# Hybrid decoder layer, recurrent branch: keys of head h+2 made beside the scan of head h, a longer planned inverse, three weight pairs, and the combination held back

## The chip, the cores and the metric

One NeuronCore of one Trainium2 chip runs one program: a whole decoder layer for 1024 tokens of width 1024, in float32. The metric is device time in microseconds (us), from the start of the execution to its end. The kernel before takes 2791.61 us, the median of three runs (2788.59 to 2793.04).

Five engines are spoken of. TensorE (PE) multiplies matrices, and loads its weights in a row of its own (PEld). VectorE (DVE) and ScalarE (ACT) work elementwise and read what TensorE leaves in PSUM. GpSimd (POOL) does little here. SyncE (SP) issues the DMAs. Each engine works through its instructions in the order of its own queue.

## The reference

```python
x = x + 0.5 * swiglu(rmsnorm(x, ffn1_norm), ...)
h = rmsnorm(x, mix_norm)
# h @ w_in gives, side by side:
#   q, k, v of branch A: attention in 3 groups of 4 heads of 64, dilations 1, 4, 16
#   q, k, v of branch B: gated delta rule, 8 heads of 128, after a causal convolution of 4 taps and silu
#   beta and decay of each head of B, the output gate of B, two merge gates
merged = sigmoid(gate_a) * (ya @ w_branch_a) + sigmoid(gate_b) * (yb @ w_branch_b)
x = x + merged @ w_out
x = x + 0.5 * swiglu(rmsnorm(x, ffn2_norm), ...)
out = rmsnorm(x, final_norm)
```

In branch A the three groups' outputs are joined by a softmax over their log-denominators. In branch B, for each head and each chunk of tokens,

```python
M = where(tri_strict, (k * beta) @ k.T * decay, 0)
u, w = solve(I + M, [v * beta, k * beta * exp(gcum)])      # unit lower triangular
# then over the chunks in turn
v_new = u - w @ state
o     = q_dec @ state + (q @ k.T * decay) @ v_new
state = state * state_dec + k_dec.T @ v_new
```

and `o` is normalised and gated. Every float32 product with a weight matrix is computed as three products of rounded parts (xH*wH + xL*wH + xH*wL).

## The kernel before, in words

**Stages.** `ffn1`, then `mixer` (attention first, then the eight recurrent heads), then `merge_out` (branch products, gates, w_out), then the second SwiGLU. `layer` runs them in order and opens the memory pools that lie between them.

**Projections.** `proj` (L206) multiplies one tile of 128 columns of `w_in` with half of the tokens: 24 matmuls of 128x512, so 48 for a tile. `load_w` (L182 to L184) brings a weight tile: a DMA into `wraw`, a ScalarE cast into `wH`, a VectorE subtraction into `wL`. Two `wraw` and four pairs of `wH` and `wL` are held.

**The planner.** In the mixer the order of TensorE's instructions is written out at build time and kept. `Weave` holds a clock in planned us: each TensorE instruction adds its planned cost (0.23 for a 128x512 matmul, 0.22 for a 128x128 one, 0.11 for a transpose). Tasks are Python generators: where one yields a number, it is due again that many planned us later. Projections are the filler: after every 2.07 planned us of them (`STRETCH`) the tasks that are due put their instructions into TensorE's stream. If an operand isn't there yet on the chip, TensorE waits; it can't take another instruction first. For the other engines a scheduler sets the order at build time by rank: attention and the combination first ("att"), then the heads in their order, then the projections ("bulk").

**A head** X of branch B goes through these tasks:

- `gdn_keys`: projection, then `gdn_conv` (ScalarE L910, L917, L920, VectorE L919), 8 planned us after each half `by_token` (transposes at L926, sum of squares L936 and L937). It starts `gdn_decay`, too.
- `gdn_decay`: the decay tile D (matmuls L993, Exp L995), of which there is one buffer. It waits until the head before has both halves of its values and its product A, and while a step of the combination is open.
- `gdn_solve`: scales D, 6 planned us later makes the products N (L1009, put out by VectorE at L1011), then `gdn_inverse_blocks`. That inverts 32x32 blocks on VectorE: N goes to DRAM and comes back into `Tm` (L1068), 60 small dependent steps (L1077, L1078, with L1090 and L1091 between), DRAM and back into `U` (L1099, L1104), a transpose into `Tm` (L1106). `Tm` has one buffer. `yield INVERSE - 5.0` and a further `yield 5.0` are the planned time of all this; INVERSE is 48.
- `gdn_merge` joins the blocks with small matmuls (L1126, L1133, L1143, L1151), a STRETCH between them; then w (L1051), then the scan.
- `gdn_queries`, `gdn_values`, `gdn_gate`: a projection each. The values' transposes wait until the head before has put out its output (`final`); once `U` is there the values are multiplied by it (L1179), which sets `solved`.
- `gdn_scan`: eight chunks in turn (L1218, L1222, L1228, L1235), a STRETCH between steps; after chunks 4 and 8 `gdn_output` is started, which 10 planned us later transposes and stores half an output.

A tile `ka` holds 128x1024; keys, scaled keys, queries, N, A, decayed keys and w of a head each take one, of nine in all.

**The combination** (`combine`) joins the attention groups in eight steps, one per 128 tokens: a dozen VectorE instructions, two transposes 12 planned us later (L866), a copy (L869). It begins 8 planned us after attention has ended, and each step waits while segments of a decay tile are open or while more than one started head lacks its values.

**The work list** in `mixer`: keys, queries, values of head 0; then for each h keys and queries of h+1, the gate of h, values of h+1, one merge gate tile. The first entry is taken once `free` says so: keys of h when head h-2 is `scanned`, the gate of h when h-1 is final, values of h when h-1 has its values. Until then one of the 16 merge gate tiles is taken as filler; when there are none, `idle` moves the clock on.

Of the kernel before, what the change touches and what calls it, by code (L numbers as in the profile page):

```python
# [9 lines left out]
F32 = mybir.dt.float32  # L10
# [6 lines left out]
P = 128  # L17
# [4 lines left out]
NT = T // P  # L22
# [46 lines left out]
def psum(C, tag):  # L69
    return C.pp.tile([P, 512], F32, name=tag, tag=tag, bufs=BANKS[tag])  # L70


@contextmanager
def band(C, name):

    saved = C.tc.cur_priority
    C.tc.cur_priority = C.bands[name]
    yield
    C.bands[name] = C.tc.cur_priority
    C.tc.cur_priority = saved  # L80
# [54 lines left out]

TILES = {"ka": 9, "xp": 2, "U": 2, "Tm": 1, "g": 1}


def t4(C, tag, dt=F32):
    return C.mx.tile([P, T + {"Tm": 32, "xp": 16}.get(tag, 0)], dt, name=tag, tag=tag, bufs=TILES[tag])

# [686 lines left out]
def combine(C):  # L830

    nc = C.nc
    while not C.attended:
        yield 1.0
    yield 8.0
    for t in range(NT):

        while C.segs or sum(not X.vals[1] for X in C.heads) > 1:
            yield 1.0
        C.combining = True  # L840
        oc = C.tp.tile([P, 792], F32, name="oc", tag="xs", bufs=2).rearrange("p (g q f) -> p g q f", g=3, q=2)
        for g in range(3):
            nc.sync.dma_start(oc[:, g], C.od[g][t * P:t * P + P])
        m, l = oc[:, :, :, 128:130], oc[:, :, :, 130:132]
        M = C.mx.tile([P, 1, 2, 2], F32, name="cM", tag="cM", bufs=2)
        e = C.mx.tile([P, 3, 2, 2], F32, name="ce", tag="ce", bufs=2)
        z = C.mx.tile([P, 3, 2, 2], F32, name="cz", tag="cz", bufs=2)
        nc.vector.tensor_tensor(out=M, in0=m[:, 0:1], in1=m[:, 1:2], op=ALU.max)
        nc.vector.tensor_tensor(out=M, in0=M, in1=m[:, 2:3], op=ALU.max)
        nc.vector.tensor_tensor(out=e, in0=m, in1=M.to_broadcast([P, 3, 2, 2]), op=ALU.subtract)  # L850
        nc.scalar.activation(e, e, AF.Exp, scale=0.125)
        nc.vector.tensor_tensor(out=z, in0=e, in1=l, op=ALU.mult)
        nc.vector.tensor_tensor(out=M, in0=z[:, 0:1], in1=z[:, 1:2], op=ALU.add)
        nc.vector.tensor_tensor(out=M, in0=M, in1=z[:, 2:3], op=ALU.add)
        nc.vector.reciprocal(M, M)
        nc.vector.tensor_tensor(out=e, in0=e, in1=M.to_broadcast([P, 3, 2, 2]), op=ALU.mult)
        for q in range(2):
            ov = oc[:, :, q, 0:128].rearrange("p g (h d) -> p g h d", d=64)
            nc.vector.tensor_tensor(out=ov, in0=ov, in1=e[:, :, q, :].unsqueeze(3).to_broadcast([P, 3, 2, 64]), op=ALU.mult)
        y = oc[:, 0, :, 0:128]  # L860
        for g in (1, 2):
            nc.vector.tensor_tensor(out=y, in0=y, in1=oc[:, g, :, 0:128], op=ALU.add)
        yield 12.0
        ps = psum(C, "tA")
        for f in range(2):
            C.weave.pe(nc.tensor.transpose(ps[:, f * P:f * P + P], y[:, f, :], C.ident), 0.11)  # L866
        C.combining = False
        yT = C.mx.tile([P, 2, P], F32, name="yT", tag="sc", bufs=6)
        nc.scalar.copy(yT, ps[:, :256].rearrange("p (f t) -> p f t", t=P))  # L869
        nc.sync.dma_start(C.yad[:, :, t * P:t * P + P], yT)  # L870
# [14 lines left out]
class Head:  # L885
# [7 lines left out]
        self.solved, self.scanned = [False] * 2, False  # L893

    @property
    def band(self):
        return f"h{self.h}"

# [41 lines left out]


def gdn_keys(C, w_in, X):
    X.ssq = C.mx.tile([P, 16], F32, name="gssq", tag="gssq", bufs=2)
    X.cl = C.mx.tile([P, 5, NT], F32, name="cl", tag="cl", bufs=2)
    X.k, X.kd = t4c(C, "ka"), t4c(C, "ka")

    def then(q):
        by_token(C, X, X.k, q, 0, X.kd)
        if q:
            yield from gdn_solve(C, X)  # L950

    C.weave.add(in_band(C, X.band, gdn_decay(C, X)), 0.0)
    gdn_conv(C, w_in, C_KB + X.h * P, 8 + X.h, X, X.k, then)
# [19 lines left out]
def gdn_decay(C, X):  # L973


    nc = C.nc
    h = X.h
    while C.combining or X.prev and not (X.prev.vals[1] and X.prev.A):
        yield 0.6
    C.segs = True  # L980
    segs = []
    for q in range(2):
        sg = C.tp.tile([P, 2, 4, P], F32R, name="seg", tag="xs", bufs=2)
        for i, gx in enumerate((C.gH, C.gL)):
            for c in range(4):
                nc.scalar.activation(sg[:, i, c, :], C.incl, AF.Copy, scale=gx[:, q * 4 + c, h:h + 1].bitcast(F32))
        segs.append(sg)
    yield 8.0
    D = C.tp.tile([P, NT, P], F32, name="Dm", tag="gB", bufs=1)
    for q, sg in enumerate(segs):  # L990
        ps = psum(C, "tA")
        for i in range(2):
            C.weave.pe(nc.tensor.matmul(ps, C.strictR, sg[:, i].rearrange("p c t -> p (c t)"), start=i == 0, stop=i == 1), 0.23)  # L993
        d = D[:, q * 4:q * 4 + 4, :]
        nc.scalar.activation(d, ps.rearrange("p (c t) -> p c t", t=P), AF.Exp)  # L995
        nc.gpsimd.affine_select(out=d, in_=d, pattern=[[0, 4], [1, P]], compare_op=ALU.is_ge, fill=0.0,
                                base=0, channel_multiplier=-1)
    X.D, C.segs = D, False


def products(C, X, src, sign):

    nc = C.nc
    dst = t4c(C, "ka")
    for q in range(2):
        ps = psum(C, "tA")
        for i in range(4):
            c = q * 4 + i
            C.weave.pe(nc.tensor.matmul(ps[:, i * P:i * P + P], X.k[:, c, :], src[:, c, :], start=True, stop=True), 0.22)  # L1009
        cs = slice(q * 4, q * 4 + 4)  # L1010
        nc.vector.scalar_tensor_tensor(dst[:, cs, :], ps.rearrange("p (c t) -> p c t", t=P), sign, X.D[:, cs, :],  # L1011
                                       op0=ALU.mult, op1=ALU.mult)
    return dst


def gdn_solve(C, X):

    nc = C.nc
    h = X.h
    while X.D is None:  # L1020
        yield 0.6
    rs, sv = rsqrt_cols(C, X.ssq[:, 0:8], 1.0, EPS, 8, "rg", w=24)
    s, nk, ks = [X.cl[:, i] for i in range(3)]
    nc.vector.tensor_tensor(out=s, in0=rs, in1=rs, op=ALU.mult)
    nc.vector.tensor_tensor(out=s, in0=s, in1=C.beta[:, :, h], op=ALU.mult)
    for q in range(2):
        d = X.D[:, q * 4:q * 4 + 4, :]
        nc.vector.tensor_tensor(out=d, in0=d, in1=s[:, q * 4:q * 4 + 4].unsqueeze(2).to_broadcast([P, 4, P]), op=ALU.mult)
    nc.vector.tensor_tensor(out=nk, in0=rs, in1=sv, op=ALU.mult)
    nc.vector.tensor_tensor(out=ks, in0=s, in1=C.eS[:, :, h], op=ALU.mult)  # L1030
    X.nk = nk
    yield 6.0
    X.N = products(C, X, X.k, -1.0)
    Tm, Um = gdn_inverse_blocks(C, X)
    yield INVERSE - 5.0
    while X.A is None:
        yield 0.6

    kg = t4c(C, "ka")
    for dst, sc in ((kg, C.eG[:, :, h]), (X.kd, ks)):  # L1040
        for q in range(2):
            cs = slice(q * 4, q * 4 + 4)
            nc.vector.tensor_tensor(out=dst[:, cs], in0=X.kd[:, cs], in1=sc[:, cs].unsqueeze(2).to_broadcast([P, 4, P]), op=ALU.mult)
    yield 5.0
    yield from gdn_merge(C, X, Tm, Um)

    X.w = t4c(C, "ka")
    for q in range(2):
        ps = psum(C, "tA")
        for i in range(4):  # L1050
            C.weave.pe(nc.tensor.matmul(ps[:, i * P:i * P + P], kg[:, q * 4 + i, :], X.U[:, q * 4 + i, :], start=True, stop=True), 0.22)  # L1051
        nc.scalar.copy(X.w[:, q * 4:q * 4 + 4, :], ps.rearrange("p (c t) -> p c t", t=P))
    yield STRETCH
    yield from gdn_scan(C, X)
# [99 lines left out]
    yield STRETCH  # L1154


INVERSE = 48.0


def gdn_values(C, w_in, X):  # L1160
# [133 lines left out]
def mixer(C, tc, I):  # L1294
# [9 lines left out]
    with tc.tile_pool(name="mx", bufs=1) as C.mx:  # L1304
# [39 lines left out]

        def free(what, h):
            if what is keys:
                return h < 2 or heads[h - 2].scanned
            if what is gdn_gate:
                return h < 1 or heads[h - 1].final[1]
            return what in (gdn_queries, gate_tile) or h < 1 or heads[h - 1].vals[1]  # L1350

        while work or gates:
            if work and free(*work[0]):
                what, h = work.pop(0)
# [78 lines left out]
            turn()  # L1433


def open_pools(C, tc, st):
    C.wbufs = (2, 4)
    C.wp = st.enter_context(tc.tile_pool(name="wp", bufs=1, reuse_waits="tile"))
    C.tp = st.enter_context(tc.tile_pool(name="tp", bufs=2, reuse_waits="tile"))


def layer(tc, I, out):
    C = Kern()
# [3 lines left out]
    with ExitStack() as st:  # L1447
# [19 lines left out]
            C.hL[a] = hp.tile([P, KT, 512], F32R, name=f"hL{a}")  # L1467

        ffn1(C, tc, I, open_h)
        open_pools(C, tc, st)  # L1470
        mixer(C, tc, I)
        C.pool_split = False
        with tc.tile_pool(name="x2", bufs=1) as xp2:
            x2 = xp2.tile([P, NT, D], F32, name="x2")
# [79 lines left out]
```

## Time and profile before

| | |
|---|---|
| three runs, us | 2788.59, 2791.61, 2793.04 |
| profiled execution, own time, us | 2792.52 |
| its span, first to last instruction, us | 2790.6 |
| mean granted TensorE clock | 0.976 |
| first SwiGLU, us of the span | 0 to 735 |
| attention | 735 to 1010 |
| recurrent heads (the last attention blocks run into it) | 1010 to 1850 |
| merge_out | 1850 to 2060 |
| second SwiGLU | 2060 to 2790 |

How to read the views that follow. The page's first part gives busy time, share of the span and count of instructions for each engine. The view by stretches gives one row per stretch of the span, in us from its start: its length, then for PE, PEld, DVE, ACT and POOL the busy time with the count in brackets, then the TensorE clock granted (1.00 is full speed), the busy share of the DMA engines, and GB/s. In the list of waits a row says which instruction of an engine waited for which other instruction: total us, times, longest. In the timeline a row is a run of like instructions: start, length, engine, line, operation, tiles written and read, shapes, count, and in square brackets the idle time before and what ended it. In a list of groups the figures behind the count are busy us, mean ns of one, and idle us before.

### The profile page before, as it was taken

The numbers are of one execution on the slowest core, as the hardware profiler recorded it, in microseconds if no ns is written. First come the engines' busy times: TensorE is split into PE (matmuls) and PEld (weight loads), VectorE is DVE, ScalarE is ACT, GpSimd is POOL, SyncE is SP. The second block draws the span as 40 slices with busy tenths as digits, with TensorE's granted clock in tenths as the row PEclk, the third lists the DMA queues.
The fourth block names the chain that finished last, engine by engine and source line by source line (L and its number), as shares of the span: only waits on it lengthen the run. The fifth ranks groups of instructions, "written<-read, shape, count | busy, mean of one in ns | idle before, by whom it ended". The sixth has DMA issues, their size and how long they took to land. (4 is left out here: it accounts for less than half of the span.)

```text
span 2790.6 us, 34448 instructions
## 1 busy us (share of the span) xinstructions
PE 2652.4 (95%) x13223; PEld 2199.6 (79%) x13223; DVE 1371.2 (49%) x3238; ACT 920.3 (33%) x1574; POOL 300.1 (11%) x256
## 2 busy tenths in 40 slices
PE   6999999999799998799899899999999999999998
PEld 5888887887688787687788777888778888888886
DVE  6443434434453458667667587345553232232325
ACT  5333332212343456344244443253441111111112
POOL 5544442001100000000000000000010000000002
PEclk9999999999899999899999999999999999999999
DMA  4322324421332222222212122255421111111111
GB/s 145 105 69 87 91 80 149 145 91 61 99 89 60 60 76 63 69 71 66 56 41 55 50 67 77 66 173 166 159 83 46 46 53 53 46 46 50 46 55 61
DMA packets 276997, 221.20 MB, mean 79 GB/s; under 512 B 38144, under 2 KB 226784, under 8 KB 276832
## 3 DMA queue, kind: packets, MB, share of 16 engines
q1 hardware_dynamic: 276832, 219.00, 26.1%
q8 instruction: 104, 1.70, 0.3%
q14 instruction: 61, 0.50, 0.1%
HBM read 173.76 MB, written 38.90 MB: 76 GB/s over the span
## 5 line engine op out<-in xcount | busy, mean ns | idle before, releaser
L206 PE MATMUL mm<-hH,wL 128*128 128x512 f32 x1440 | 589.9, 410 | 0.0
L206 PE MATMUL mm<-hL,wH 128*128 128x512 f32 x1440 | 567.5, 394 | 0.0
L206 PE MATMUL mm<-hH,wH 128*128 128x512 f32 x1440 | 567.4, 394 | 0.0
L183 ACT CAST wH<-wraw 128x1024 fp32r<-128x1024 f32 (+1 forms) x189 | 197.3, 1047 | 747.7 <-PE mm L206 328.4
L184 DVE TENSOR_TENSOR wL<-wraw,wH 128x1024 fp32r<-128x1024 f32 (+1 forms) x189 | 230.5, 1222 | 213.9 <-ACT wH L183 204.8
L206 PEld LDWEIGHTS mm<-hL,wH 128*128 128x128 f32 x1440 | 273.9, 190 | 60.7
L206 PEld LDWEIGHTS mm<-hH,wL 128*128 128x128 f32 x1440 | 274.1, 190 | 59.7 <-issue 6.0
L206 PEld LDWEIGHTS mm<-hH,wH 128*128 128x128 f32 x1440 | 274.8, 191 | 50.4
L206 PE MATMUL tC<-hH,wL 128*128 128x512 f32 x416 | 161.8, 389 | 0.0
L206 PE MATMUL tC<-hL,wH 128*128 128x512 f32 x416 | 161.8, 389 | 0.0
L206 PE MATMUL tC<-hH,wH 128*128 128x512 f32 x416 | 161.8, 389 | 0.0
L263 DVE TENSOR_TENSOR sg<-sg,tC 128x512 f32<-128x512 f32 x44 | 30.3, 688 | 247.9 <-PE tC L206 247.9
L239 POOL TENSOR_TENSOR xg<-x,gB 128x1024 f32<-128x1024 f32 x16 | 38.3, 2395 | 602.3 <-DVE x L1427 357.0
L387 DVE TENSOR_TENSOR wL<-wS,wH 128x1024 fp32r<-128x1024 f32 x44 | 63.3, 1438 | 79.2 <-ACT wH L386 77.9
L1482 POOL TENSOR_TENSOR y<-x,gB 128x1024 f32<-128x1024 f32 x8 | 19.1, 2388 | 706.3 <-DVE x L294 706.3
L206 PEld LDWEIGHTS tC<-hL,wH 128*128 128x128 f32 x416 | 78.1, 188 | 16.3
L206 PEld LDWEIGHTS tC<-hH,wL 128*128 128x128 f32 x416 | 78.2, 188 | 16.2
L206 PEld LDWEIGHTS tC<-hH,wH 128*128 128x128 f32 x416 | 78.0, 187 | 16.1
L919 DVE SCALAR_TENSOR_TENSOR ka<-xp,cw,ka 128x512 f32<-128x512 f32 x96 | 72.5, 755 | 13.1 <-ACT ka L917 11.9
L455 POOL TENSOR_TENSOR su<-su,sg 128x512 f32<-128x512 f32 x42 | 64.3, 1551 | 86.5 <-DVE su L429 76.7
L386 ACT CAST wH<-wS 128x1024 fp32r<-128x1024 f32 x44 | 46.3, 1052 | 78.1 <-PE tC L397 37.5
L568 PE MATMUL mm<-wH,hidH 128*128 128x512 f32 x176 | 69.3, 394 | 2.6 <-DVE x L570 1.8
(405 smaller groups left out, 5347.6 us busy)
## 6 DMA issues: line engine op xcount, KB each, us to landing
wraw<-in_w_in_dram SPq DMA_DIRECT2D x64, 512.0 KB, 4.0
wraw<-in_ffn_w_gate_dram SPq DMA_DIRECT2D x46, 512.0 KB, 3.9
wraw<-in_ffn_w_up_dram SPq DMA_DIRECT2D x46, 512.0 KB, 4.0
wraw<-in_ffn_w_down_dram SPq DMA_DIRECT2D x44, 512.0 KB, 3.6
wraw<-hd SPq DMA_DIRECT2D x22, 512.0 KB, 4.9
hd<-su SPq DMA_DIRECT2D x42, 256.0 KB, 3.2
wraw<-in_w_branch_b_dram SPq DMA_DIRECT2D x16, 512.0 KB, 4.3
wraw<-in_w_out_dram SPq DMA_DIRECT2D x16, 512.0 KB, 3.7
```

Of the source, the lines that this page charges most:

```text
L183: nc.scalar.copy(H[:, :width], raw[:, :width])
L184: (nc.gpsimd if C.pool_split else nc.vector).tensor_tensor(out=L[:, :width], in0=raw[:, :width], in1=H[:, :width].bitcast(F32), op=ALU.sub ...
L206: ins = nc.tensor.matmul(ps, w[:, k, :], x[:, k, :], start=k == 0 and i == 0, stop=k == kt - 1 and i == 2)
L239: nc.gpsimd.tensor_tensor(out=xs, in0=x_t, in1=gB, op=ALU.mult)
L263: nc.vector.tensor_tensor(out=sg, in0=sg, in1=pu, op=ALU.mult)
L386: nc.scalar.copy(H[:, :n], srcs)
L387: eng.tensor_tensor(out=L[:, :n], in0=srcs, in1=H[:, :n].bitcast(F32), op=ALU.subtract)
L455: C.nc.gpsimd.tensor_tensor(out=out, in0=out, in1=sg, op=ALU.mult)
L568: nc.tensor.matmul(ps, h[:, m], w, start=i == 0, stop=i == len(seq) - 1)
L919: nc.vector.scalar_tensor_tensor(o, x, w, o, op0=ALU.mult, op1=ALU.add)
L1482: nc.gpsimd.tensor_tensor(out=y, in0=x2[:, t], in1=gF, op=ALU.mult)
```

## The change

Seven edits go together.

1. `TILES`: eleven `ka` buffers in place of nine; `gssq` and `cl`, small tiles of a head, get three buffers in place of two.
2. `free`: keys of head h may start when head h-2 has its solved values (its scan is about to run), no longer when it is scanned. Queries of h, which were always free, now need head h-2 scanned.
3. `gdn_solve`: the products N of head h, and so its inverse, wait until head h-2 is scanned.
4. `INVERSE` is 62 planned us in place of 48.
5. `combine` starts when head 1 has its merged `U`, and each step also waits while a started head could have its decay tile made but hasn't.
6. The mixer holds three pairs `wH` and `wL` in place of four.
7. The pool for `tp` is opened before the weights' pool; the mixer has a weights' pool of its own, closed after it, and a new one with four pairs is opened behind it.

```diff
-TILES = {"ka": 9, "xp": 2, "U": 2, "Tm": 1, "g": 1}
+TILES = {"ka": 11, "xp": 2, "U": 2, "Tm": 1, "g": 1}
...
 def combine(C):
-    while not C.attended:
+    while not C.attended or len(C.heads) < 2 or C.heads[1].U is None:
         yield 1.0
-    yield 8.0
     for t in range(NT):
-        while C.segs or sum(not X.vals[1] for X in C.heads) > 1:
+        while C.segs or any(X.D is None and X.ready for X in C.heads) or sum(not X.vals[1] for X in C.heads) > 1:
             yield 1.0
...
     @property
+    def ready(self):
+        return not self.prev or self.prev.vals[1] and self.prev.A is not None
...
 def gdn_keys(C, w_in, X):
-    X.ssq = C.mx.tile([P, 16], F32, name="gssq", tag="gssq", bufs=2)
-    X.cl = C.mx.tile([P, 5, NT], F32, name="cl", tag="cl", bufs=2)
+    X.ssq = C.mx.tile([P, 16], F32, name="gssq", tag="gssq", bufs=3)
+    X.cl = C.mx.tile([P, 5, NT], F32, name="cl", tag="cl", bufs=3)
...
 def gdn_decay(C, X):
-    while C.combining or X.prev and not (X.prev.vals[1] and X.prev.A):
+    while C.combining or not X.ready:
...
 def gdn_solve(C, X):
     yield 6.0
+    while X.prev and X.prev.prev and not X.prev.prev.scanned:
+        yield 0.6
     X.N = products(C, X, X.k, -1.0)
...
-INVERSE = 48.0
+INVERSE = 62.0
...
         def free(what, h):
             if what is keys:
+                return h < 2 or heads[h - 2].solved[1]
+            if what is gdn_queries:
                 return h < 2 or heads[h - 2].scanned
             if what is gdn_gate:
                 return h < 1 or heads[h - 1].final[1]
-            return what in (gdn_queries, gate_tile) or h < 1 or heads[h - 1].vals[1]
+            return what is gate_tile or h < 1 or heads[h - 1].vals[1]
...
-def open_pools(C, tc, st):
-    C.wbufs = (2, 4)
+def open_weights(C, tc, st, bufs):
+    C.wbufs = bufs
     C.wp = st.enter_context(tc.tile_pool(name="wp", bufs=1, reuse_waits="tile"))
-    C.tp = st.enter_context(tc.tile_pool(name="tp", bufs=2, reuse_waits="tile"))
...
         ffn1(C, tc, I, open_h)
-        open_pools(C, tc, st)
-        mixer(C, tc, I)
+        C.tp = st.enter_context(tc.tile_pool(name="tp", bufs=2, reuse_waits="tile"))
+        with ExitStack() as own:
+            open_weights(C, tc, own, (2, 3))
+            mixer(C, tc, I)
+        open_weights(C, tc, st, (2, 4))
```

More of the change, by code (lines that the diff above doesn't have):

```diff
@@ L895, in band @@
     @property
+    def ready(self):
+        return not self.prev or self.prev.vals[1] and self.prev.A is not None
+    @property
     def band(self):
```

## The prediction

> **What bounds the kernel now.** I read the page first, then the busy times by stage, then the list of who TensorE waits for in the one stage that the change reorders, and last the rows of the waits themselves. The page, then four stretches (PE busy, PEld, DVE, ACT, POOL, granted clock, DMA share, GB/s):
>
> ```profile
> span 2790.6 us, 34448 instructions
> PE 2652.4 (95%) x13223; PEld 2199.6 (79%) x13223; DVE 1371.2 (49%) x3238; ACT 920.3 (33%) x1574; POOL 300.1 (11%) x256
> ```
> ```profile
> 735.00:1010.00 275.00, 267.15 (x1462) 219.53 (x1462) 121.86 (x330) 107.79 (x301) 1.50 (x3) 0.98 0.29 77
> 1010.00:1850.00 840.00, 767.35 (x4520) 644.08 (x4521) 560.54 (x1816) 363.84 (x688) 23.84 (x53) 0.95 0.24 68
> 1850.00:2060.00 210.00, 206.08 (x919) 168.24 (x918) 119.81 (x224) 92.35 (x122) 19.25 (x8) 0.99 0.45 145
> 2060.00:2790.00 730.00, 717.15 (x3168) 592.84 (x3166) 244.66 (x407) 110.23 (x138) 19.10 (x8) 0.99 0.17 52
> ```
>
> TensorE bounds the kernel. Its work is the same before and after the change, so only its idle time and its clock can move. The recurrent stage (1010 to 1850) holds 840 - 767.35 = 72.65 us of idle time and the lowest clock, 0.95; attention holds 7.85 us, the output stage 3.92. The waits of TensorE in the recurrent stage (total, times, longest):
>
> ```profile
> PE tM L1126 <- DVE Tm L1106: 53.5, 7, 18.5
> PE tA L866 <- DVE ka L1011: 4.8, 1, 4.8
> PE tA L926 <- ACT ka L920: 4.1, 2, 2.3
> ...
> PE tA L926 <- ACT yT L869: 0.8, 2, 0.5
> ```
>
> 53.5 of the 72.65 us are one wait: the first matmuls of a merge (L1126) stand in TensorE's fixed order before the inverse's last step on VectorE (the transpose L1106) is done. Next, TensorE's rows for the products that start an inverse (L1009, heads 1 to 7), and for the merges (heads 0 to 7; in brackets the idle time before):
>
> ```profile
> 1104.48 1.06 PE L1009 MATMUL tA<-ka 128*128 128x128 f32 x8
> ...
> 1252.02 1.95 PE L1009 MATMUL tA<-ka 128*128 128x128 f32 x16
> ...
> 1330.94 2.00 PE L1009 MATMUL tA<-ka 128*128 128x128 f32 x16
> ...
> 1431.72 2.01 PE L1009 MATMUL tA<-ka 128*128 128x128 f32 x16
> ...
> 1506.12 2.00 PE L1009 MATMUL tA<-ka 128*128 128x128 f32 x16
> ...
> 1606.41 2.01 PE L1009 MATMUL tA<-ka 128*128 128x128 f32 x16
> ...
> 1684.46 1.95 PE L1009 MATMUL tA<-ka 128*128 128x128 f32 x16
> ```
> ```profile
> 1122.64 1.27 PE L1126 MATMUL tM<-Tm,ka 32*32 32x32 f32 x32
> ...
> 1129.42 1.14 PE L1143 MATMUL tM<-Tm,ka 64*64 64x64 f32 x16
> ...
> 1185.42 1.72 PE L1126 MATMUL tM<-Tm,ka 32*32 32x32 f32 x32 [18.47 <-DVE Tm L1106]
> 1306.09 1.09 PE L1126 MATMUL tM<-Tm,ka 32*32 32x32 f32 x32 [1.54 <-DVE Tm L1106]
> 1392.05 1.14 PE L1126 MATMUL tM<-Tm,ka 32*32 32x32 f32 x21 [9.65 <-DVE Tm L1106]
> 1486.50 1.09 PE L1126 MATMUL tM<-Tm,ka 32*32 32x32 f32 x32 [2.54 <-DVE Tm L1106]
> 1566.90 1.30 PE L1126 MATMUL tM<-Tm,ka 32*32 32x32 f32 x24 [9.30 <-DVE Tm L1106]
> 1663.18 1.06 PE L1126 MATMUL tM<-Tm,ka 32*32 32x32 f32 x19 [4.80 <-DVE Tm L1106]
> 1745.54 1.19 PE L1126 MATMUL tM<-Tm,ka 32*32 32x32 f32 x22 [7.20 <-DVE Tm L1106]
> ```
>
> From products to merge, heads 1 to 7 needed 80.9, 54.1, 61.1, 54.8, 60.8, 56.8 and 61.1 us. The planner had set aside 16 products of 0.22, then 48 - 5, then 5: 51.5 planned us. Head 5 without its wait comes to 60.8 - 9.3 = 51.5, so a planned us is about a real one here.
>
> **The change, part by part.** *62 for 48 in INVERSE.* The merge moves 14 planned us back, to 65.5 us after the products. Against the times just listed that leaves 11.4, 4.4, 10.7, 4.7, 8.7 and 4.4 us to spare for heads 2 to 7, and head 1 lacks 15.4. Head 1 has its own limit: the tile Tm exists once, so its inverse starts only when the merge of head 0 has read it last (L1143, ended at 1130.6), 54.9 us before head 1 was ready. That merge moves too, by 14 less the 5.6 us of waits at the combination (4.8 + 0.8), which no longer stands there: 1139.0. In those 54.9 us VectorE also ran two steps of the combination; from the groups of VectorE between 1131 and 1186 their two largest lines are
>
> ```profile
> L859 DVE TENSOR_TENSOR oc<-oc,ce 128x384 f32<-128x384 f32 x4 | 2.0, 549 | 0.0
> ...
> L862 DVE TENSOR_TENSOR oc<-oc 128x256 f32<-128x256 f32 x4 | 1.7, 418 | 0.0
> ```
>
> together 3.7 us, gone once the combination is held back. So head 1 is ready at 1139.0 + 51.2 = 1190 and due at 1185.42 - 18.47 - 5.6 + 14 = 1175.4: it waits 15 us still. For the six others I add 4 us together, since three of them keep under 5 us and every inverse will now run beside a scan. Waits at merges: 53.5 to 19, a gain of 34.5.
>
> *The clock.* After a wait TensorE works on at a lower granted clock. Three stretches behind merges (heads 1, 2 and 7):
>
> ```profile
> 1185.40:1191.40 6.00, 5.98 (x44) 5.24 (x45) 1.13 (x3) 0.40 (x2) 0.00 (x0) 0.50 0.00 0
> 1306.00:1311.00 5.00, 4.91 (x43) 3.98 (x44) 2.11 (x4) 2.59 (x4) 0.64 (x1) 0.66 0.06 12
> ...
> 1745.50:1752.00 6.50, 6.46 (x67) 5.12 (x68) 0.85 (x2) 0.59 (x1) 0.00 (x0) 0.56 0.11 41
> ```
>
> The share withheld is 3.0, 1.7 and 2.9 us, 2.5 in the mean, for seven merges 17.5 at most. The small matmuls suffer less (32 of them took 1.72 us at 0.50 and 1.27 at head 0), so I estimate 12, of which 3 stay with head 1 and the short waits: a gain of 9. The Trainium skill (TensorE: Matmul & The Clock Gate, section HAM oscillation) puts the rule as no pauses over about 3.4 us; by it the wait of head 2, 1.54 us, would have cost no clock, and the gain would be some 2 us less. The trace disagrees: 0.66 was granted behind that wait.
>
> *Keys of h+2 beside the scan of h, two more ka tiles, third buffers for gssq and cl.* The same projection and convolution, issued earlier; the products still wait for the scan's end. Before, the scan of head 4 ended at
>
> ```profile
> 1546.95 0.38 PE L1235 MATMUL tC<-v,ka 128*128 128x128 f32 x2
> ...
> 1802.88 0.38 PE L1235 MATMUL tC<-v,ka 128*128 128x128 f32 x2
> ...
> 1847.35 0.61 PE L206 MATMUL mm<-mH,wH 128*128 128x512 f32 x2
> ```
>
> and the products of head 6 followed 59.5 us later, 50 without head 5's wait. Now the decay tile decides: the output of h takes 10 planned us, which lets the values of h+1 through, then 8 for the decay and 6 for the scaling, with polls about 27. So the chain over two heads loses 23 us and gains 14: it gets 9 us shorter, and the 14 us aren't paid by TensorE. Were the keys not earlier, the reserve would have to cover them: after the last scan (1802.9) TensorE still had 44.5 us of gate tiles before the output stage (1847.35).
>
> What the earlier keys do cost lies on VectorE, busy 560.54 of 840 us: the convolution has lower rank there than the scan and the inverse beside which it now runs, and TensorE turns the result 8 planned us after each half. The nearest rows are of the values of head 6, convolved beside an inverse; ScalarE's copy that begins the second half, and the Silu that ends it:
>
> ```profile
> 1635.93 0.57 ACT L910 COPY xp<-mm 128x512 f32<-128x512 f32 x1
> ...
> 1642.57 0.63 ACT L920 ACTIVATE vT<-vT 128x512 f32<-128x512 f32 x1 [0.85 <-DVE vT L919]
> ```
>
> That is 7.3 us of 8. I take 3 us of new waits in all (between 0 and 12 halves of 2.3, the longest wait for L920 so far).
>
> *Combination held back.* It removes 5.6 us of waits near heads 0 and 1; its eight steps come later, with their VectorE work ahead of everything. I keep 3 us of gain (between 5.6 and 0).
>
> *Three weight pairs; weights pool opened anew after the mixer; tp opened first.* ScalarE's waits, its last cast ahead of the output stage, and TensorE's wait at the mixer's opening:
>
> ```profile
> ACT wH L183 <- PE mm L206: 84.5, 35, 8.1
> ```
> ```profile
> 1836.44 1.05 ACT L183 CAST wH<-wraw 128x1024 fp32r<-128x1024 f32 x1 [4.31 <-PE mm L206]
> ```
> ```profile
> PE mm L663 <- ACT wH L183: 6.1, 1, 6.1
> ```
>
> TensorE's own list names neither wH nor wL in this stage, though the casts wait for its matmuls: the next pair is split while a whole tile of 48 matmuls runs, so the third pair costs nothing. The cast at 1836.44 serves the matmul at 1847.35, about 9 us ahead. If the new pool's first pair lies over the pair of the last gate tile, that lead is gone and TensorE waits for a split; the nearest row for a stage that opens with weights missing is the 6.1 us. I take 2.5 (0 to 6.1 at each of the two borders).
>
> Sum against the profiled run's own 2792.52 us (its span and 1.92 around it): -34.5 - 9 - 3 + 3 + 2.5 = -41, so 2751.5; the median of the three runs is 0.9 lower, hence **2750**.
>
> **The rivals.** *All waits go* (chance 0.12): head 1's inverse, free of the combination, is in time as well. Gain 53.5 + 12 + 5.6 = 71: 2721. Against it stands the single Tm.
>
> *The 62 are used up* (0.16): scan, convolution and up to three combination steps inside each inverse make heads 2 to 7 late by 3.5 us each, with 1.5 of clock: 30 us where I counted 5, so 2775. For it: 4.4 us to spare at heads 3 and 7. Against: heads 3, 5 and 7 already ran beside a scan.
>
> *The waits only slide* (0.06): with one Tm, a merge 14 us later lets the next inverse start 14 us later. It decides where products of neighbours stand under about 63 us apart. Before, they stood 78.9, 100.8, 74.4, 100.3 and 78.1 apart from head 2 on, and a head's five tiles keep that. Nothing gained: 2790.
>
> *Slower: the keys' turn waits behind the inverse* (0.09). The twelve halves of heads 2 to 7 are convolved two ranks below the inverse; if each is 5 us late, with 1.5 us of clock, that is 78 us in place of my 3: 2825. From 2.2 us late (with the clock 3.7, times 12) it outweighs the gain. For it: 7.3 of 8 us. Against: that second half was still in time, amid an inverse.
>
> **How the numbers follow.** The forecast has 0.57, the rivals 0.12, 0.16, 0.06 and 0.09. The range runs from the first rival to the second, 2721 to 2776, and leaves out 0.15. A measurement here tells about 0.2% (5.6 us) from no change: faster 0.57 + 0.12 + 0.16 = 0.85, same 0.06, slower 0.09.
>
> **What would show it.** Right: L1126 <- L1106 falls from 53.5 to some 19 us, nearly all at head 1; the clock of the stage rises above 0.95; keys' convolutions stand inside the scans; gate tiles still follow the last scan. Wrong: waits at L1126 for heads 2 to 7 over 3 us each, L926 <- L920 far above 4.1 us, a wait of L206 for wH or wL at the mixer's end, or TensorE idle with no gate tile left.

## The result, and the profile after

The changed kernel takes 2755.18 us, the median of four runs (2753.07 to 2761.43), against 2791.39 (2788.59 to 2793.04) for the kernel before: a ratio of 0.9875, 95% interval 0.9856 to 0.9894. Its profiled execution took 2753.14 us, with a span of 2751.1, 39.5 us shorter than before's 2790.6.

The page of the changed kernel, first part:

```profile
span 2751.1 us, 34433 instructions
PE 2644.0 (96%) x13223; PEld 2190.9 (80%) x13223; DVE 1380.5 (50%) x3238; ACT 920.8 (33%) x1574; POOL 299.8 (11%) x256
```

Its four stages by stretches, the columns as before:

```profile
735.00:1010.00 275.00, 268.62 (x1465) 220.45 (x1464) 118.99 (x329) 106.22 (x301) 0.55 (x2) 0.98 0.28 74
1010.00:1810.00 800.00, 756.69 (x4504) 633.20 (x4503) 568.72 (x1814) 364.07 (x685) 23.49 (x53) 0.97 0.25 72
1810.00:2030.00 220.00, 214.13 (x967) 175.31 (x967) 125.27 (x232) 98.71 (x128) 19.26 (x8) 1.00 0.46 145
2030.00:2750.00 720.00, 708.21 (x3124) 585.73 (x3122) 238.45 (x394) 103.76 (x129) 19.11 (x8) 0.99 0.16 50
```

The recurrent stage is 40 us shorter, and TensorE's idle time in it went from 72.65 to 800 - 756.69 = 43.3 us. Whom TensorE waits for in that stage of the changed kernel:

```profile
PE tA L930 <- ACT ka L924: 16.7, 8, 3.8
PE mm L206 <- issue: 7.3, 1, 7.3
PE tM L1132 <- DVE Tm L1112: 5.7, 1, 5.7
PE tA L865 <- issue: 3.5, 1, 3.5
```

Lines have moved: L1132 and L1112 are before's L1126 and L1106 (a merge, and the inverse's last transpose), L930 and L924 its L926 and L920 (the turn of a convolved half, and its Silu), L865 its L866 (the combination's transposes). The wait at the merges fell from 53.5 to 5.7 us. In its place stand 16.7 us at the turns, 4.1 before, and a new wait of 7.3 us at L206.

The first matmul of the mixer and the first of `merge_out` (it reads mH), and the last row of the last scan, of the changed kernel:

```profile
734.06 0.57 PE L663 MATMUL mm<-wH,hH 128*128 128x272 f32 x1
...
1768.57 0.38 PE L1241 MATMUL tC<-v,ka 128*128 128x128 f32 x2
...
1806.22 1.19 PE L206 MATMUL mm<-mH,wH 128*128 128x512 f32 x2 [7.29 <-issue]
```

So the mixer takes 1072.2 us; before, it took 1847.35 - 737.48 = 1109.9:

```profile
737.48 0.57 PE L663 MATMUL mm<-wH,hH 128*128 128x272 f32 x1
```

Of the 39.5 us of span, 37.7 lie in the mixer. The first SwiGLU, which nobody touched, was 3.4 us shorter in this execution, and what follows the mixer 1.6 longer. The last scan now ends 34 us earlier, 31 if counted from the mixer's start, and 30 us of gate tiles still follow it (to 1798.9).

The whole mixer as a stretch, before and after:

```profile
737.48:1847.35 1109.87, 1030.73 (x5963) 860.67 (x5964) 678.34 (x2140) 467.37 (x980) 24.39 (x55) 0.96 0.25 70
734.06:1806.22 1072.16, 1022.49 (x5964) 852.04 (x5964) 684.84 (x2142) 467.63 (x982) 24.04 (x55) 0.98 0.26 72
```

TensorE's idle time in it fell from 79.1 to 49.7 us, by 29.5: merges -47.8, turns +12.6, the border +7.3, the combination -2.1 (5.6 to 3.5), other waits +0.5. Its busy time fell by 8.2 us: the same work done faster, at a mean clock of 0.98 in place of 0.96.

### The profile page after: what moved, and what is told of

It reads as the page before. It is cut to its first block, busy times and chain, and to the rows that moved or that the text cites. A ratio compares the mean times of both kernels' runs of the same rounds, so it can differ in the third digit from the quotient of the medians.

```text
span 2751.1 us, 34433 instructions
## 1 busy us (share of the span) xinstructions
PE 2644.0 (96%) x13223; PEld 2190.9 (80%) x13223; DVE 1380.5 (50%) x3238; ACT 920.8 (33%) x1574; POOL 299.8 (11%) x256
## 5 line engine op out<-in xcount | busy, mean ns | idle before, releaser
L206 PE MATMUL mm<-hH,wL 128*128 128x512 f32 x1440 | 588.5, 409 | 0.1
L206 PE MATMUL mm<-hL,wH 128*128 128x512 f32 x1440 | 565.1, 392 | 0.0
L206 PE MATMUL mm<-hH,wH 128*128 128x512 f32 x1440 | 564.7, 392 | 0.0
L206 PEld LDWEIGHTS mm<-hH,wL 128*128 128x128 f32 x1440 | 273.2, 190 | 59.5 <-issue 6.0
L206 PEld LDWEIGHTS mm<-hL,wH 128*128 128x128 f32 x1440 | 272.0, 189 | 60.5
L206 PEld LDWEIGHTS mm<-hH,wH 128*128 128x128 f32 x1440 | 273.1, 190 | 49.6
L206 PE MATMUL tC<-hH,wL 128*128 128x512 f32 x416 | 161.8, 389 | 0.0
L206 PE MATMUL tC<-hL,wH 128*128 128x512 f32 x416 | 161.8, 389 | 0.0
L206 PE MATMUL tC<-hH,wH 128*128 128x512 f32 x416 | 161.8, 389 | 0.0
L387 DVE TENSOR_TENSOR wL<-wS,wH 128x1024 fp32r<-128x1024 f32 x44 | 63.3, 1439 | 79.1 <-ACT wH L386 77.9
L206 PEld LDWEIGHTS tC<-hH,wH 128*128 128x128 f32 x416 | 78.2, 188 | 16.3
L206 PEld LDWEIGHTS tC<-hL,wH 128*128 128x128 f32 x416 | 78.1, 188 | 16.2
L206 PEld LDWEIGHTS tC<-hH,wL 128*128 128x128 f32 x416 | 78.0, 187 | 16.1
L923 DVE SCALAR_TENSOR_TENSOR ka<-xp,cw,ka 128x512 f32<-128x512 f32 x96 | 73.2, 764 | 5.3 <-ACT ka L921 4.7
```

What stands on the lines that cost most here:

```text
L206: ins = nc.tensor.matmul(ps, w[:, k, :], x[:, k, :], start=k == 0 and i == 0, stop=k == kt - 1 and i == 2)
L387: eng.tensor_tensor(out=L[:, :n], in0=srcs, in1=H[:, :n].bitcast(F32), op=ALU.subtract)
L923: nc.vector.scalar_tensor_tensor(o, x, w, o, op0=ALU.mult, op1=ALU.add)
```

## The experiments

Times are us, ratios are against the kernel before in the same session; the other columns are from the profiled execution. The mixer's length runs from its first matmul to the first that reads mH. Its start differs by up to 4.3 us from execution to execution, which shifts the end of the last scan with it.

| kernel | median (range, runs) | ratio, 95% | mixer starts | mixer | last scan ends |
|---|---|---|---|---|---|
| before | 2791.39 (2788.59-2793.04, 4) | 1 | 737.5 | 1109.9 | 1803.3 |
| the change | 2755.18 (2753.07-2761.43, 4) | 0.9856-0.9894 | 734.1 | 1072.2 | 1769.0 |
| inv62_only | 2760.10 (2757.39-2762.30, 4) | 0.9878-0.9907 | 737.3 | 1077.1 | 1799.6 |
| after_inv48 | 2802.59 (2801.95-2809.60, 4) | 1.0035-1.0067 | 736.6 | 1118.9 | 1789.7 |
| comb_only | 2782.41 (2780.77-2784.16, 5) | 0.9955-0.9980 | 736.1 | 1101.2 | 1793.2 |
| inv62_comb | 2748.63 (2747.31-2749.12, 5) | 0.9831-0.9858 | 735.4 | 1063.7 | 1787.8 |
| after_oldcomb | 2751.81 (2749.23-2752.41, 4) | 0.9843-0.9870 | 735.4 | 1068.5 | 1770.4 |
| split_only | 2800.57 (2790.73-2803.27, 10) | 1.0024-1.0046 | 737.0 | 1117.1 | 1801.7 |
| one_pool | 2747.62 (2746.09-2749.33, 4) | 0.9830-0.9857 | 737.6 | 1064.5 | 1772.3 |
| one_more_gate | 2752.43 (2748.64-2754.57, 4) | 0.9852-0.9879 | 734.9 | 1067.3 | 1787.9 |
| inv59_comb | 2753.58 (2751.71-2755.21, 4) | 0.9848-0.9881 | 736.7 | 1069.6 | 1794.6 |
| turn11 | 2771.55 (2770.10-2772.87, 4) | 0.9919-0.9949 | 738.4 | 1087.0 | 1798.6 |
| one_pool_turn | 2742.73 (2740.57-2748.25, 4) | 0.9814-0.9844 | 736.4 | 1062.6 | 1781.5 |
| comb_last | 2740.81 (2738.95-2745.91, 5) | 0.9817-0.9844 | 736.1 | 1060.0 | 1778.5 |

### Which edit brings the gain

**inv62_only**: the kernel before with one number changed.

```diff
-INVERSE = 48.0
+INVERSE = 62.0
```

> The kernel before with INVERSE 62 in place of 48 and nothing else. Theory A (the planned 48 us were too short, and the filler covers 14 more): waits at L1126 fall from 53.5 to about 20 us, nearly all at head 1, the clock gives back some 9, TensorE has gate tiles left behind the last scan; about 2749 us. Rival B (the longer inverse pays only because the keys come earlier): the chain over two heads grows by 14 us, the gate tiles run out before the last scan ends, and TensorE is idle for about 40 us there; about 2790 us.

It took 2760.1 us, 30 less than before: that number alone brings most of the gain. Its waits:

```profile
PE tM L1126 <- DVE Tm L1106: 11.3, 1, 11.3
PE tA L926 <- DVE ka L1011: 9.0, 3, 3.5
```

Only head 1 still waits at its merge, as Theory A has it, though the time is 11 us above A's. Rival B's 40 us of idle time at the end don't come: one wait of 3.2 us stands there. But the last scan ends at 1799.6, hardly earlier than before, and the gate tiles last only to 1811.2: of 44.5 us of filler behind the last scan, 11.6 are left. The longer planned inverse was paid out of that reserve.

**after_inv48**: the changed kernel with the old number.

```diff
-INVERSE = 62.0
+INVERSE = 48.0
```

> The changed kernel with INVERSE 48. Theory A: the waits at the merges return in full (about 50 us in place of 5.7), and the keys' turns (16.7 us) and the border (7.3 us) stay: 2800 to 2810 us. Rival B (the earlier keys are themselves worth time): products come some 20 us earlier for each pair of heads, more gate tiles are left, waits at the merges stay under 25 us: about 2770 us.

It is slower than before, 2802.59. The first line of its waits:

```profile
PE tM L1132 <- DVE Tm L1112: 51.6, 8, 12.7
```

The merges wait as before; the earlier keys take nothing from that. They do end the last scan sooner (1789.7 against 1803.3), so there is more filler behind it, but filler at the end shortens nothing while TensorE isn't dry there. Its mixer is 9 us longer than before's; at the border it waits 9.3 us.

**comb_only** and **inv62_comb**: the kernel before with the combination held back (edit 5 and the property `ready` that it needs), without and with the 62.

```diff
-    while not C.attended:
+    while not C.attended or len(C.heads) < 2 or C.heads[1].U is None:
         yield 1.0
-    yield 8.0
...
-        while C.segs or sum(not X.vals[1] for X in C.heads) > 1:
+        while C.segs or any(X.D is None and X.ready for X in C.heads) or sum(not X.vals[1] for X in C.heads) > 1:
```

> The kernel before with the combination held back as in the change, and nothing else. Theory A (two combination steps lie in head 1's inverse): head 1's wait falls from 18.5 to about 12 us, the 4.8 us at L866 go there and 3 come back later: about 2782 us. Rival (the combination's VectorE work costs the same wherever it stands): 2791 us.

> The kernel before with INVERSE 62 and the combination held back: the change without the earlier keys, the extra tiles and the pools. Theory A (the two planned times do nearly all, the earlier keys earn about what the border and the turns cost): about 2752 us, as the changed kernel or a few us faster. Rival B (without the earlier keys the gate tiles run out and TensorE stands at the end of the mixer): over 2762 us, with a wait of over 10 us behind the last scan.

Held back alone it brings 8.7 us, the time that Theory A gave, but not by A's terms: head 1 still waits 15.0 us, not 12, and the combination's own transposes 7.7 (6.2 and 1.5) in place of 5.6. Of the 8.6 us by which its mixer is shorter 4.5 are idle time; the other 4.1 are faster matmuls, which no row here explains. Together with the 62 it takes 2748.63. These two edits give the whole gain: the kernel without earlier keys, more tiles and new pools is 6.6 us below the full change (all its runs lie below all of the change's, though the intervals of the ratios touch).

**after_oldcomb**: the changed kernel with before's start and conditions of `combine`.

```diff
-    while not C.attended or len(C.heads) < 2 or C.heads[1].U is None:
+    while not C.attended:
         yield 1.0
+    yield 8.0
...
-        while C.segs or any(X.D is None and X.ready for X in C.heads) or sum(not X.vals[1] for X in C.heads) > 1:
+        while C.segs or sum(not X.vals[1] for X in C.heads) > 1:
```

> The changed kernel with the combination started as before, 8 planned us after attention. Theory A: head 1 waits about 11 us in place of 5.7, the 4.8 us at L866 are back, and the turns at heads 2 and 3, which stand behind combination steps on VectorE, lose 5 of their 16.7 us: about 2762 us. Rival: held back, the combination only moves its waits, 2755 us.

2751.81, below both forecasts: in the changed kernel, holding the combination back brings nothing. By the waits: head 1's merge waits 9.0 instead of 5.7 and the combination's own transposes 4.8 instead of 3.5, but the turns for ScalarE's Silu wait 12.3 (9.9 and 2.4) instead of 16.7, and the border 5.6 instead of 7.3. What it saves at head 1 it gives back at the turns.

With the 62 in all four kernels there is a square: 2760.10 us with neither, 2748.63 with the combination held back, 2751.81 with the earlier keys, tiles and pools, 2755.18 with both. Each alone brings 8 to 11 us, both together only 5. So the earlier keys aren't idle as such: beside an early combination they pay, though the new pool's cost is in their 2751.81. Which of those edits does it was not run apart.

### The border

**split_only**: the kernel before, with its four pairs, but the mixer's weights' pool closed behind the mixer and opened anew (edit 7 alone).

```diff
-        open_pools(C, tc, st)
-        mixer(C, tc, I)
+        C.tp = st.enter_context(tc.tile_pool(name="tp", bufs=2, reuse_waits="tile"))
+        with ExitStack() as own:
+            open_weights(C, tc, own, (2, 4))
+            mixer(C, tc, I)
+        open_weights(C, tc, st, (2, 4))
```

> The kernel before with a weights pool of its own for the mixer (still four pairs), closed and opened anew behind it, tp opened first, and nothing else. If the 7.3 us at the border come from the new pool: the first branch weights are fetched only after the last gate tile, TensorE waits about 7 us there with 3 us of clock behind it, about 2800 us. If they come from the shorter tail of gate tiles: no wait at the border and 2791 us.

It costs 10 us (2800.57; nine of the ten runs took 2798.86 to 2803.27, one 2790.73), and TensorE waits 8.1 us at the border. The changed kernel's border, with SyncE's queue (SPq), where a row is a DMA being issued:

```profile
1798.53 0.39 PE L206 MATMUL mm<-hH,wL 128*128 128x512 f32 x1
1799.00 0.59 ACT L880 COPY gt<-mm 128x512 f32<-128x512 f32 x1 [0.16 <-PE mm L206]
1799.62 0.32 SPq L881 DMA_DIRECT2D sgbd<-gt  x1
1799.98 0.94 SPq L182 DMA_DIRECT2D wraw<-in_w_branch_a_dram  x2
...
1805.07 1.04 ACT L183 CAST wH<-wraw 128x1024 fp32r<-128x1024 f32 x1 [1.27 <-DMA wraw<-in_w_branch_a_dram]
1806.15 2.56 DVE L184 TENSOR_TENSOR wL<-wraw,wH 128x1024 fp32r<-128x1024 f32 x2 [1.53 <-ACT wH L183]
```

The first weights of `merge_out` aren't even loaded until the last gate tile is done and stored: 1799.98 for the load, 5 us to the cast, 1 to the matmul. The records don't tell whether the load stands behind the store in SyncE's queue or waits for the old pool's last reader; the new pool brings it either way.

**one_pool**: the changed kernel with one pool of three pairs kept open, and the fourth pair in a small pool of its own, opened behind the mixer.

```diff
+    C.nw = getattr(C, "nw", 0) + 1
+    fourth = C.wq and not to and C.nw % 4 == 0
-    H, L = to or [C.wp.tile([P, SLOT], F32R, name=t, tag=t, bufs=C.wbufs[1]) for t in ("wH", "wL")]
+    H, L = to or [(C.wq.tile([P, SLOT], F32R, name=t, tag=t, bufs=1) if fourth else
+                   C.wp.tile([P, SLOT], F32R, name=t, tag=t, bufs=C.wbufs[1])) for t in ("wH", "wL")]
...
-        with ExitStack() as own:
-            open_weights(C, tc, own, (2, 3))
-            mixer(C, tc, I)
-        open_weights(C, tc, st, (2, 4))
+        open_weights(C, tc, st, (2, 3))
+        mixer(C, tc, I)
+        C.wq = st.enter_context(tc.tile_pool(name="wq", bufs=1, reuse_waits="tile"))
```

> The changed kernel, but the mixer's weights pool of three pairs stays open to the end, and a fourth pair lies in a small pool of its own opened behind the mixer; no pool is closed and opened anew between them. If the 7.3 us at the border come from the new pool, they go, with some 2 us of clock behind them: about 2746 us. If the border waits for something else (the stores of the last gate tile, the loads of the branch's input), it stays: 2755 us.

2747.62. At its border TensorE goes on without a pause:

```profile
1801.83 0.39 PE L209 MATMUL mm<-hH,wL 128*128 128x512 f32 x1
1802.06 0.62 PE L209 MATMUL mm<-mH,wH 128*128 128x512 f32 x2
```

Three pairs in the mixer cost nothing (behind its opening no wait of TensorE there is for wH or wL); the pool opened anew cost 7.6 us. And one_pool, with the earlier keys, stands level with inv62_comb, without them (2748.63).

### What the earlier keys are worth

inv62_comb has no filler left: its last scan and its last gate tile end together, at 1787.8 and 1787.6. The rows after that:

```profile
1787.40 0.39 PE L1239 MATMUL tC<-v,ka 128*128 128x128 f32 x2
1793.91 1.09 PE L930 MATMUL tA<-ident,vb 128*128 128x128 f32 x4 [6.12 <-DVE vb L1264]
1799.11 2.01 PE L206 MATMUL mm<-mH,wH 128*128 128x512 f32 x3 [4.11 <-ACT mH L213]
```

**one_more_gate** puts the last gate tile there a second time.

```diff
+    gates += gates[-1:]
```

> The kernel inv62_comb (the kernel before with 62 planned us for the inverse and the combination held back), in which the last gate tile is computed twice: 48 more matmuls, 11.1 us of TensorE's work by that tile's own rows. Theory: inv62_comb has used up the gate tiles when its last scan ends, and waits 6.1 us at the last output's turn and 4.1 us for ScalarE at the stage's end, because the chain of the heads sets the end; then the added work mostly fills those 10 us, and the time goes from 2748.6 to at most 2753. Rival: TensorE's work sets the end, and those waits are there whatever stands between; then all 11 us are added, to about 2760.

2752.43, 3.8 us more; the mixer is 3.6 longer:

```profile
1797.56 0.60 PE L930 MATMUL tA<-ident,vb 128*128 128x128 f32 x4
1802.22 1.19 PE L206 MATMUL mm<-mH,wH 128*128 128x512 f32 x2 [4.06 <-ACT mH L213]
```

TensorE's busy time in the mixer rose by 9.6 us, 6.0 of which fill what was idle time (the pause of 6.1 us fell to 0.9); 3.6 move the end. So in inv62_comb the chain of the heads sets the mixer's end, and TensorE is dry for 10.2 us, of which the 4.1 stay with the added tile in place, too. The earlier keys cure that (one_pool: no pause at the border, 30 us of filler), and pay for it at the turns: 16.7 us in one_pool against 4.9 for the same line in inv62_comb. Over the whole mixer one_pool is idle for 42.3 us against 46.5, but its matmuls take 1022.2 us against 1017.3: 4.2 saved, 4.9 paid, level. That the slower matmuls are those behind the turns' waits is likely, not shown.

**inv59_comb** tried to end that dry stretch sooner: inv62_comb with 59.

```diff
-INVERSE = 62.0
+INVERSE = 59.0
```

> The kernel before with the combination held back and INVERSE 59 (in place of 62 in the run inv62_comb). There TensorE was dry at the mixer's end: the last scan ended with no gate tile left, and two waits of 6.1 and 4.1 us followed, while six of eight merges had more than 3 us to spare. If the chain of the heads sets that end, 3 planned us less for each inverse bring it forward by some 10 us: the two waits shrink to 4 us at most, the merges of heads 3 and 7 wait under 1 us each, and the time is about 2741 us. If the waits at the end belong to the border itself (loads and splits of the output stage), they stay, and the time is 2748 us.

A miss: 2753.58, and the last scan ends later, by 5.5 us if counted from the mixer's start. Its waits:

```profile
PE tA L930 <- ACT ka L924: 10.7, 6, 3.7
...
PE tA L865 <- DVE ka L1015: 6.2, 1, 6.2
...
PE mm L206 <- ACT mH L213: 4.1, 1, 4.1
```

Against inv62_comb, with 4.9 us in the first line and 0.5 for L865, the three planned us moved other steps into one another. A number of the plan changes the whole order behind it, and these two small waits change by some 6 us each with it.

### The turns

VectorE's queue ahead of the second longest turn of the changed kernel (queries of head 2; L858 belongs to the combination, L1015 to products, L921 and L923 are the convolution), and the turn:

```profile
1226.18 0.72 ACT L921 ACTIVATE ka<-xp,cw 128x512 f32<-128x512 f32 x1
...
1228.20 1.02 DVE L858 TENSOR_TENSOR oc<-oc,ce 128x384 f32<-128x384 f32 x2
...
1230.51 1.02 DVE L858 TENSOR_TENSOR oc<-oc,ce 128x384 f32<-128x384 f32 x2
...
1232.73 0.75 DVE L923 SCALAR_TENSOR_TENSOR ka<-xp,cw,ka 128x512 f32<-128x512 f32 x1
...
1234.87 0.68 DVE L1015 SCALAR_TENSOR_TENSOR ka<-tA,Dm 128x512 f32<-128x512 f32 x1
...
1236.07 0.75 DVE L923 SCALAR_TENSOR_TENSOR ka<-xp,cw,ka 128x512 f32<-128x512 f32 x1
...
1237.53 1.12 PE L930 MATMUL tA<-ident,ka 128*128 128x128 f32 x4 [3.09 <-ACT ka L924]
```

The convolution's three VectorE steps, 0.75 us each, run from 1232.73 to 1236.82, 4.1 us: parts of an output and of head 2's own products go between them. ScalarE's part (L921) was done at 1226.9, 5.8 us before the first of them, and what VectorE did in between is mostly two steps of the combination. The longest turn (keys of head 3, 3.8 us) has another cause: between its convolution's steps stand the last transpose of head 2's inverse and the scaling behind it (L1049), from 1290.27 to 1293.89:

```profile
1290.27 1.24 DVE L1112 STREAM_TRANSPOSE Tm<-U 128x1024 f32<-128x1024 f32 x1
1291.43 1.26 DVE L1049 TENSOR_TENSOR ka<-ka,ex 128x512 f32<-128x512 f32 x2
1292.60 1.29 DVE L1049 TENSOR_TENSOR ka<-ka,cl 128x512 f32<-128x512 f32 x2
```

**turn11** gives every turn three planned us more.

```diff
-        C.weave.add(in_band(C, X.band, then(q)), 8.0)
+        C.weave.add(in_band(C, X.band, then(q)), 11.0)
```

> The changed kernel with the turns of a convolved half 11 planned us after it in place of 8. If the 16.7 us of waits of the turns for the Silu come from a convolution that takes more than 8 us, they fall to about 5 us, the clock gives back some 4, and the time is about 2740 us. If TensorE waits there because VectorE or ScalarE as a whole is behind, the wait moves to the next reader (L1013 or L1132), and the time stays at 2755 us.

A miss: 2771.55, 16 us slower than the change.

```profile
PE tM L1132 <- DVE Tm L1112: 14.7, 2, 12.6
...
PE tA L1185 <- issue: 7.1, 2, 5.1
PE tA L930 <- DVE ka L1015: 6.3, 2, 3.9
...
PE tA L930 <- ACT ka L924: 2.7, 2, 1.9
```

The turns' own wait shrinks from 16.7 to 2.7, as meant, but the chain of every head gets longer, and the last scan ends 25 us later, counted from the mixer's start. Filler isn't what is short: 17.7 us of it still follow the last scan. Other steps were moved into waits: head 1's merge waits 12.6, and 7.1 and 6.3 us are new. The mixer is idle for 10.7 us more than in the change, and its matmuls take 4.1 us longer.

**one_pool_turn** is one_pool with the 11 for heads 2 and later alone.

```diff
-        C.weave.add(in_band(C, X.band, then(q)), 8.0)
+        C.weave.add(in_band(C, X.band, then(q)), 11.0 if X.h > 1 else 8.0)
```

> The run one_pool with the turns of a convolved half 11 planned us after it, for heads 2 to 7 only; heads 0 and 1, whose delay brought head 1's wait back to 12.6 us in the run turn11, keep 8. If the turns' waits are a matter of 3 planned us, 16.7 us become about 5 and the time is about 2738 us. If VectorE and ScalarE as a whole are behind at those places, the waits move to other readers, and the time is 2747 us or more.

2742.73; the interval of its ratio, 0.9814 to 0.9844, lies below the change's. The turns' wait fell to 5.4 us as meant, but head 1's merge waits 10.4 in place of 5.7, though heads 0 and 1 kept the 8. Against one_pool's 2747.62 the intervals overlap, and the mixer is only 1.9 us shorter.

**comb_last** also ranks the combination, on VectorE and ScalarE, behind all heads.

```diff
-    C.bands = {"att": base, "bulk": base + 400000}
+    C.bands = {"att": base, "bulk": base + 400000, "comb": base + 300000}
...
-        C.weave.add(in_band(C, "att", combine(C)), 0.0)
+        C.weave.add(in_band(C, "comb", combine(C)), 0.0)
```

> The kernel one_pool_turn (one weights pool kept open, keys' and queries' turns of heads 2 and later 3 planned us later), with the combination's steps ranked on VectorE and ScalarE behind the work of all heads instead of among it; TensorE's planned order stays. Theory: the waits left in the first heads (3.9 at the turn of the decay tile, 2.3 at a convolution's turn, 3.3 at a matmul on cM, and the clock behind them) come from two held-back combination steps, some 7 us of VectorE's work each, that stand ahead of convolution and inverse. With the combination behind them those waits fall to under 2 us each, and the time to about 2735 us against one_pool_turn's 2742.7. Rival: the combination's own transposes stand at a fixed place in TensorE's order, so the wait only moves to them (4 us or more there) and the time stays at 2740 to 2745.

```profile
PE tM L1135 <- DVE Tm L1115: 10.5, 1, 10.5
PE tA L868 <- issue: 4.8, 2, 2.7
...
PE tA L933 <- DVE ka L1018: 3.5, 3, 2.3
PE tA L933 <- ACT ka L927: 3.1, 3, 1.8
...
PE tA L868 <- DVE oc L864: 1.4, 1, 1.4
```

2740.81: the rival had it. The waits for convolutions get a little smaller (5.4 to 3.1), a wait of 3.3 us on cM goes, and 6.2 us at the combination's own transposes (L868) take their place. A step of the combination is 3.3 us of VectorE's work in this trace, not 7. By the intervals one_pool, one_pool_turn and comb_last can't be told apart two by two (though all runs of comb_last lie below all of one_pool's), but the last two are faster than both the kernel before (by 1.7%) and the change.

## Why the prediction was right, and where its terms were off

The forecast (2750) lies 5 us below the measured 2755.18, and its mechanism held: the longer planned inverse takes the merges' wait away, TensorE doesn't pay for it with idle time at the end, a filler of gate tiles still follows the last scan. The terms, predicted against measured in the profiled execution:

- **Merges: -34.5 against -47.8.** Heads 2 to 7 don't wait at all; their inverses end 2.1 to 16.4 us ahead of the merge. The four us "for the six others" weren't needed. Head 1 waits 5.7 us, not 15. The step that was most off is "That merge moves too, by 14 less the 5.6 us of waits at the combination ...: 1139.0". Head 0's merge, its reading of Tm, and the start of head 1's, in the changed kernel:

```profile
1130.44 1.14 PE L1149 MATMUL tM<-Tm,ka 64*64 64x64 f32 x16
...
1179.54 1.73 PE L1132 MATMUL tM<-Tm,ka 32*32 32x32 f32 x32 [5.71 <-DVE Tm L1112]
```

  The changed kernel's mixer starts 3.4 us earlier in this execution, so 3.4 us are to be added before these times are compared with the forecast's. The last reader of Tm ended at 1131.6, which makes 1135.0, not 1139.0: 4.0 us earlier. From Tm's release to head 1's merge there are 47.9 us, not 51.2: 3.3 less. Head 1 was due at 1179.5 - 5.7 = 1173.8, which makes 1177.2, not 1175.4: 1.8 later. These three are the 9 us between 15 and 5.7. As to the first: from head 0's products to its merge there are 71.4 us before, 81.3 in inv62_only, 72.3 in inv62_comb and 75.0 here. So the 14 planned us were about 10 real ones there, and the combination's steps, put at 5.6, took 6 to 9.

- **Clock: -9 against -8.2.**

- **Turns: +3 against +12.6.** Inside the bounds (0 to 27.6), but the step "That is 7.3 us of 8. I take 3 us of new waits" sized them too low: that row was of a convolution beside an inverse alone, and the bounds counted the keys' halves only. Of the eight turns that wait, 2.1 us each in the mean, six are queries' (10.5 of the 16.7 us). In the changed kernel steps of the combination, products and an output can stand ahead of a convolution besides. The rival *slower: the keys' turn waits behind the inverse* holds for the longest turn, keys of head 3, but it wanted twelve such halves at 5 us.

- **Combination: -3 against -2.1**, here. What I didn't see: alone on the kernel before it brings 8.7 us, and inside the changed kernel nothing; there its steps stand ahead of convolutions, and the turns wait 16.7 us in place of 12.3.

- **Border: +2.5 against +7.3**, and some 2 us of clock behind it (below). The step "If the new pool's first pair lies over the pair of the last gate tile ... TensorE waits for a split" was too mild: not the split alone is late but the load ahead of it. "The third pair costs nothing" held.

- **The keys.** "Were the keys not earlier, the reserve would have to cover them" is what inv62_only and inv62_comb show, and the reserve does cover them, all but 3.2 us at the end of the one and 10.2 at the end of the other. That step was right, and I still didn't price it: beside a combination held back, the chain that the earlier keys shorten ends in filler that nothing waits for, and past those 10 us the turns cost what it saves.

Two of the signs that were to show the forecast wrong did come: the turns' wait far above 4.1 us, and a wait of L206 at the mixer's end. Together they cost 20 of the 48 us that the merges gained, and left the mechanism standing.

Of the rivals, *all waits go* is refuted by head 1 (5.7 us here, 10.4 in one_pool_turn), *the 62 are used up* by the slack of heads 2 to 7, and *the waits only slide* by the last scan's end. That the sum, -41 against a span of -39.5, came so near is in part luck, errors of opposite sign: the gain at the merges was put 13 us too low, the cost of turns and border together 14 too low. The first SwiGLU's 3.4 us, which no term covers, helped as well. The median fell by 36.2.

## What to carry to other kernels

Where an engine's order is fixed at build time, a planned duration that is too short costs a wait each time, and one that is long enough takes its price from the filler: measure the real durations, set the plan to them, and look at how much filler is left behind the last dependent step before paying for a shorter chain. But a changed number also moves other steps into one another: three planned us more at the turns cost 16 us here with filler to spare. A buffer pool closed and opened anew between two stages can take away the prefetch across the border, here 7.6 to 10 us. Edits that each gain alone can take back one another's gain, so run them apart and in pairs.

## What the runs showed that was not expected

The clock behind short waits follows no plain length of pause. The changed kernel behind turns that waited 3.79, 1.70 and 2.72 us, and behind the border's 7.29:

```profile
1296.40:1301.50 5.10, 5.05 (x14) 4.19 (x15) 3.37 (x19) 3.19 (x6) 0.00 (x0) 0.50 0.02 6
1483.20:1488.00 4.80, 4.80 (x61) 3.93 (x61) 2.64 (x6) 1.20 (x2) 0.00 (x0) 1.00 0.17 27
1646.60:1651.60 5.00, 4.99 (x25) 4.16 (x26) 2.20 (x7) 0.60 (x1) 0.00 (x0) 0.50 0.34 77
1806.20:1811.00 4.80, 4.76 (x12) 3.35 (x13) 4.53 (x6) 3.65 (x6) 0.00 (x0) 0.58 0.96 350
```

2.72 us of waiting cost half the clock for 5 us, 1.70 us none, where 1.54 us in the kernel before were followed by 0.66 (neither the 2.72 nor the 1.54 has another wait over 0.1 us in the 15 us ahead of it); the border's 4.8 us at 0.58 are 2 us lost. The Trainium skill (TensorE: Matmul & The Clock Gate, section HAM oscillation) allows pauses up to about 3.4 us; by it only the first and the last of these four would have cost clock, and the trace disagrees at the third.
